# First mixer of a decoder trunk: GpSimd without products and weight parts, triangles inverted in blocks of eight rows, weight parts 512 columns wide in three tiles

## The chip, the core and the metric

The kernel runs on one core of a Trainium2 chip. The core has TensorE (PE, with its weight loads shown apart as PEld), VectorE (DVE), ScalarE (ACT), GpSimd (POOL) and SyncE (SP, which issues the DMAs here). Each engine works through a queue of its own in order. The metric is device microseconds of one execution; lower is better. Times of instructions are from one profiled execution.

## What is computed

Two layers on x of 256 tokens by 2048: an RWKV-7 mixer, then differential attention, each followed by a gated MLP and by layer norms. The change is in the mixer. Cut to what matters:

```
xr, xw, xk, xv, xa, xg = (x + xx * mu[i] for i in range(6))     # xx: the token before, less x
r, k, v = xr @ w_rkv[0], xk @ w_rkv[1], xv @ w_rkv[2]
w = -softplus(-(w0 + tanh(xw @ w1) @ w2)) - 0.5
a = sigmoid(a0 + (xa @ a1) @ a2);   g = sigmoid(xg @ g1) @ g2
kk = normalized(k * k_k) per head;   k = k * (1 + (a - 1) * k_a);   decay = exp(-exp(w))
for t:  S = S * decay_t + (S a_t) b_t^T + v_t k_t^T;   y_t = S r_t     # a_t = -kk, b_t = kk * a
h = ((group_norm(y) * lnx_g + lnx_b + bonus) * g) @ w_o
```

Everything is float32. The step over t is not run token by token: the 256 tokens of a head are four chunks of 64, and in each chunk the effect of the (S a_t) b_t^T terms is the inverse of a triangular 64x64 matrix with ones on its diagonal.

## The kernel before

A float32 weight is cut into two parts in a rounded format, hi (an ACT cast of raw) and lo (raw less hi, a subtraction), and three products, hi with both parts of x and lo with the first, give a dense product on PE. `weights` (by way of `chunk`, L199) does it for a block of 128 outputs: one DMA brings `raw` with four k-tiles (512 columns), and for each HCH = 2 k-tiles (256 columns) ACT casts hi (L210) and DVE or POOL subtracts lo (L213). Where `pool_every` is n, every nth lo goes to POOL: every third in the first stage, every fourth in the groups. The tiles for raw, hi and lo come from rings; the ring "0" has (3, 4, 4) tiles, and the first stage has a second one, "v", with (6, 6, 6); blocks take turns between the rings that are open.

The first stage of the mixer (`rwkv`, to about 160 us) makes V from 16 blocks of weights, the first factors of the low-rank gates, and the mixes of x: for each mix and k-tile a product `mx` (L773) and a hi and lo part (L191, L192). Then the 32 heads go as 8 groups of four heads (two k-tiles), in a pipeline (`Groups.pipeline`): while group i is in `chain` (the recurrence over the four chunks) and `outputs`, group i+1 is in `lanes` (the triangles), i+2 in `front` (decays, normalization, the products AR, KB and M) and i+3 in `products` (its k and r, 4 blocks of 16 k-tiles). Near the end `early` puts part of w_o in the place of `products`. The generators are stepped by turns (`_together`, with the numbers of PACE), and the framework then sets the order of each engine's queue.

The steps that the change touches:

- POOL's products: Lx = L - sw (L1107), a = kk * a (L1122), one half of KB (L1130; DVE makes the other at L1129), r = r * k (L1159), KB times pc (L1198), and in `outputs` bon * rs (L1382) and V = y + bon (L1388).
- `lanes` inverts each triangle from the inside: the matrices go to DRAM and come back as `Ml`, one block of 16 rows to a partition and step; fifteen pairs of a product (L1209) and a reduce (L1211) on DVE fill Tl; Tl goes by DRAM to W1, 32 rows at a time. Then PE joins blocks of 16 into 32 (transpose L1227, matmuls L1233, copy to Z, matmuls L1240, copy to W1) and blocks of 32 into 64 (L1245 to L1267). The result stands in M, which `chain` reads.
- `chain` has for each chunk three hand-overs from PE and back: R (L1049), UV (L1049) and S (L1354).

Of the kernel before, what the change touches and what calls it, by code (L numbers as in the profile page):

```python
# [74 lines left out]
def _const_layout():  # L75
    at, n = {}, 0
    for name, w in (("ident", P), ("onesd", P)):
        at[name] = n
        n += w
    base = n  # L80
    for name, w in (("bd1", P), ("cent", P), ("mask", P), ("reset", T)):
# [12 lines left out]
def _constants():  # L94
    c = np.zeros((P, NCONST), np.float32)

    def put(name, a):
        c[:a.shape[0], CCOL[name]:CCOL[name] + a.shape[1]] = a

    eye = np.eye(P, dtype=np.float32)  # L100
    bd = np.kron(np.eye(2, dtype=np.float32), np.ones((64, 64), np.float32))
    put("ident", eye)
    put("bd1", bd)
    put("cent", eye - bd / 64)
    put("ones", np.ones((P, P), np.float32))
# [3 lines left out]
    put("mask", np.concatenate([s < t, s <= t], 1).astype(np.float32))  # L109
    reset = np.ones((P, T), np.float32)  # L110
# [12 lines left out]
    return c  # L123


class Trunk:
    def __init__(self, ctx, tc, a):
        self.ctx, self.tc, self.nc, self.a = ctx, tc, tc.nc, a
        nc = self.nc
# [18 lines left out]

    def weight_pools(self, ctx, name, bufs=(3, 4, 4)):
        w = tuple(ctx.enter_context(self.tc.tile_pool(name=f"{n}{name}", bufs=b))  # L150
                  for n, b in zip(("raw", "hi", "lo"), bufs))
        self.wp.append(w)
        ctx.callback(self.wp.remove, w)
# [46 lines left out]
    def chunk(self, src, k0, m, wp, pool=False):  # L200
        nc = self.nc
        wraw, whi, wlo = wp
        raw = wraw.tile([P, WCH * P], F32, name="raw")
        nc.sync.dma_start(out=raw[:, :m * P], in_=src[:, k0 * P:(k0 + m) * P])
        for k in range(0, m, HCH):
            s = min(HCH, m - k)
            r = raw[:, k * P:(k + s) * P]
            hi = whi.tile([P, HCH * P], F32R, name="hi")
            lo = wlo.tile([P, HCH * P], F32R, name="lo")
            nc.scalar.copy(out=hi[:, :s * P], in_=r)  # L210
            self.nw += 1
# [748 lines left out]
class Groups:  # L960
# [10 lines left out]
    def open(self):  # L971
# [103 lines left out]
    def front(self, g):  # L1075
# [51 lines left out]
        for par in range(2):  # L1127
            k_, a_, e_ = (self.half(x, par) for x in (ck, ca, ce))
            nc.vector.tensor_tensor(out=self.half(KB[:, :, par, :], par), in0=k_, in1=e_, op=ALU.mult)  # L1129
            nc.gpsimd.tensor_tensor(out=self.half(KB[:, :, 1 - par, :], par), in0=a_, in1=e_, op=ALU.mult)  # L1130
        nc.vector.scalar_tensor_tensor(out=AR[:, :, 0, :], in0=c3, scalar=-1.0, in1=_ch(_fl(Lx)), op0=ALU.mult,
# [26 lines left out]

        nc.gpsimd.tensor_tensor(out=r, in0=r, in1=k, op=ALU.mult)  # L1159
        for jj, j in js:  # L1160
# [17 lines left out]
    def lanes(self, g):  # L1178
# [15 lines left out]
        for q in range(2):  # L1194
            r = slice(64 * q, 64 * q + 64)
            nc.gpsimd.memset(Tl[r].rearrange("p a b -> p (a b)")[:, 8 * q:8 * q + 7 * 17 + 1:17], 1.0)

        nc.gpsimd.tensor_tensor(out=KB.rearrange("p c a s -> p c (a s)"), in0=KB.rearrange("p c a s -> p c (a s)"),  # L1198
                                in1=pc.rearrange("p j c o -> p (j c) o").broadcast_to([P, GT * NC, 2 * C]),
                                op=ALU.mult)  # L1200
        yield
        for u in range(0, GT * NC, 4):
# [11 lines left out]
        for q in range(2):  # L1214
            nc.sync.dma_start(out=self.dram(d2, 0, ((DBL, 64), (C, 8), (1, 16)), at=8 * C * q),
                              in_=Tl[64 * q:64 * q + 64])
        for par in range(2):
# [27 lines left out]
        nc.vector.transpose(out=T2.rearrange("p u t -> p (u t)"), in_=W1.rearrange("p u t -> p (u t)"))  # L1245
        Z2 = g1.tile([P, 8, 32], F32, name="Z2")
        ps = self.pst()
# [117 lines left out]
    def outputs(self, g):  # L1365
# [15 lines left out]
        nc.tensor.matmul(ps, lhsT=t.x("bd1"), rhs=_fl(y2), start=True, stop=True)  # L1381
        nc.gpsimd.tensor_tensor(out=bon, in0=bon, in1=rs, op=ALU.mult)  # L1382
        nc.vector.tensor_scalar(out=_fl(y2), in0=ps, scalar1=1.0 / 64, scalar2=GN_EPS, op0=ALU.mult, op1=ALU.add)
# [80 lines left out]
```

## Time and profile before

| | |
|---|---|
| timed runs, three | 2576.1 us median, 2573.64 to 2580.8 |
| the profiled execution | 2568.52 us, of which its span is 2566.5 |
| busy share of the span | PE 96%, DVE 80%, ACT 64%, POOL 15% |
| mean granted TensorE clock | 0.981 of 2.4 GHz |
| lo parts | 2984 on DVE, 144 on POOL |

The page gives busy shares over the whole span; the mixer is the first quarter of it and has other limits than the rest, so it is read by stretches. A matmul's end is modelled, so PE's busy time says little of how densely it is fed; the distance of starts says more.

### The profile page before, as it was taken

To read this page: it belongs to the slowest core of one execution; us is meant where nothing else is said; L and a number is where in the kernel's file an instruction comes from. 1 tells how busy PE (TensorE), PEld (TensorE's weight loads), DVE (VectorE), ACT (ScalarE), POOL (GpSimd) and SP (SyncE) were. 2 spreads that over 40 slices of the span, in tenths; PEclk is the share of its full clock that TensorE was granted. 3 is DMA by queue.
4 is the path that set the end of the run, shared out by engine and by line. 5 is a ranking of instruction groups with operands and counts; after the bars stand their busy time and mean duration, and the time that the engine had idled before them with its cause. 6 is when DMAs were issued, how large, how long until landed. Compare 5 with 4: busy or idle time off the path is not lost.

```text
span 2566.5 us, 54810 instructions
## 1 busy us (share of the span) xinstructions
PE 2468.5 (96%) x17598; PEld 2171.5 (85%) x17598; DVE 2053.8 (80%) x5100; ACT 1645.2 (64%) x4318; POOL 390.7 (15%) x456
## 2 busy tenths in 40 slices
PE   7999989899899999999999999999999999999996
PEld 6888778767788888888889899998888888888886
DVE  8977888887897777777777877779997777777776
ACT  5765555644576666666566766666676666666664
POOL 4343344332400000000111200003300000000111
PEclk9999999999999999999999999999999999999998
DMA  6544334344466555556766555556465555566664
GB/s 191 175 129 116 102 104 108 99 121 124 125 187 192 190 190 190 190 189 184 225 190 183 156 171 171 171 167 196 145 199 188 188 188 188 188 186 185 189 190 127
DMA packets 285186, 429.63 MB, mean 167 GB/s; under 512 B 69081, under 2 KB 91617, under 8 KB 284897
## 3 DMA queue, kind: packets, MB, share of 16 engines
q1 hardware_dynamic: 284896, 426.14, 55.0%
q8 instruction: 137, 2.24, 0.4%
q14 instruction: 153, 1.25, 0.2%
HBM read 421.03 MB, written 6.57 MB: 167 GB/s over the span
## 4 chain that ended last, share of the span: by engine, by line
PE 74%; DVE 4%; ACT 1%; issue 1%; DMA 1%; POOL 0%; ACTq 0%; DVEq 0%; SPq 0%; POOLq 0%
PE psd L225 42%; PE psd L226 21%; PE psd L293 1%; PE psd L291 1%; PE psd L292 1%; DVE lo L213 1%; PE psd L897 1%; PE psd L896 1%; PE psd L898 1%; PE lnst L345 1%; PE psd L221 1%; PE psd L223 1%; PE psd L222 1%; DMA raw<-in_rw_o 0%; PE pss L656 0%
## 5 line engine op out<-in xcount | busy, mean ns | idle before, releaser
L210 ACT CAST hi<-raw 128x256 fp32r<-128x256 f32 (+1 forms) x3128 | 1231.1, 405 | 676.5 <-PE psd L225 461.2
L213 DVE TENSOR_TENSOR lo<-raw,hi 128x256 fp32r<-128x256 f32 (+1 forms) x2984 | 1287.5, 442 | 404.4 <-ACT hi L210 369.4
L225 PE MATMUL psd<-S,hi 128*128 128x512 f32 x3004 | 1056.7, 396 | 0.4 <-ACT hi L210 0.4
L226 PE MATMUL psd<-S,lo 128*128 128x256 f32 x3004 | 842.2, 280 | 4.4 <-DVE lo L213 3.8
L225 PEld LDWEIGHTS psd<-S,hi 128*128 128x128 f32 x3004 | 566.0, 188 | 132.5 <-ACT hi L210 1.2
L226 PEld LDWEIGHTS psd<-S,lo 128*128 128x128 f32 x3004 | 565.8, 188 | 5.9 <-DVE lo L213 4.5
L225 PE MATMUL psd<-hs,hi 128*128 128x512 f32 x1290 | 451.4, 394 | 0.1
L226 PE MATMUL psd<-hs,lo 128*128 128x256 f32 x1290 | 361.5, 280 | 0.0
L225 PEld LDWEIGHTS psd<-hs,hi 128*128 128x128 f32 x1290 | 241.8, 187 | 56.5 <-ACT hi L210 1.0
L226 PEld LDWEIGHTS psd<-hs,lo 128*128 128x128 f32 x1290 | 243.1, 188 | 0.4 <-DVE lo L213 0.3
L363 POOL COPY ln_acc<-X 128x256 f32<-128x256 f32 x4 | 2.1, 528 | 1230.9 <-DVE X L397 1230.9
L213 POOL TENSOR_TENSOR lo<-raw,hi 128x256 fp32r<-128x256 f32 x144 | 130.4, 913 | 301.2 <-ACT hi L210 244.1
L223 PE MATMUL psd<-S,lo 128*128 128x256 f32 x480 | 140.6, 293 | 13.8 <-DVE lo L213 8.4
L221 PE MATMUL psd<-S,hi 128*128 128x256 f32 x480 | 141.6, 295 | 0.9 <-ACT hi L210 0.5
L222 PE MATMUL psd<-S,hi 128*128 128x256 f32 x480 | 141.4, 295 | 0.0
L223 PEld LDWEIGHTS psd<-S,lo 128*128 128x128 f32 x480 | 92.8, 193 | 22.3 <-DVE lo L213 12.8
L225 PE MATMUL psd<-S1r,hi 128*128 128x512 f32 x276 | 109.9, 427 | 1.4 <-ACT o_rs L1049 0.7
L370 POOL TENSOR_TENSOR ln_acc<-ln_acc,X 128x256 f32<-128x256 f32 x49 | 40.9, 834 | 402.4 <-DVE X L409 389.1
L221 PEld LDWEIGHTS psd<-S,hi 128*128 128x128 f32 x480 | 92.5, 193 | 5.7 <-ACT hi L210 1.5
L222 PEld LDWEIGHTS psd<-S,hi 128*128 128x128 f32 x480 | 92.8, 193 | 2.9 <-issue 2.7
L221 PE MATMUL psd<-S1r,hi 128*128 128x256 f32 x284 | 87.2, 307 | 1.4 <-ACT S1r L191 0.9
L897 PE MATMUL psd<-S,lo 128*128 128x258 f32 x256 | 75.4, 295 | 10.1 <-DVE lo L213 10.1
(297 smaller groups left out, 3823.5 us busy)
## 6 DMA issues: line engine op xcount, KB each, us to landing
raw<-in_ff_up SPq DMA_DIRECT2D x676, 256.0 KB, 3.4
raw<-in_ff_down SPq DMA_DIRECT2D x320, 256.0 KB, 3.0
raw<-in_rkv SPq DMA_DIRECT2D x192, 256.0 KB, 3.5
raw<-in_da_qk SPq DMA_DIRECT2D x122, 256.0 KB, 3.4
raw<-in_da_v SPq DMA_DIRECT2D x64, 256.0 KB, 3.1
raw<-in_da_o SPq DMA_DIRECT2D x64, 256.0 KB, 3.5
raw<-in_rw_o SPq DMA_DIRECT2D x50, 256.0 KB, 3.5
raw<-in_ff_down SPq DMA_DIRECT2D x32, 192.0 KB, 2.7
```

What stands on the lines that cost most here:

```text
L210: nc.scalar.copy(out=hi[:, :s * P], in_=r)
L213: eng.tensor_tensor(out=lo[:, :s * P], in0=r, in1=hi[:, :s * P].bitcast(F32), op=ALU.subtract)
L221: nc.tensor.matmul(ps[:, :T], lhsT=hi, rhs=xs[:, :T], start=first, stop=False)
L222: nc.tensor.matmul(ps[:, :T], lhsT=hi, rhs=xs[:, T:], start=False, stop=False)
L223: nc.tensor.matmul(ps[:, :T], lhsT=lo, rhs=xs[:, :T], start=False, stop=last)
L225: nc.tensor.matmul(ps, lhsT=hi, rhs=xs, start=first, stop=False)
L226: nc.tensor.matmul(ps[:, T:], lhsT=lo, rhs=xs[:, :T], start=False, stop=last)
L291: nc.tensor.matmul(o, lhsT=xh, rhs=hi, start=k == 0 and b == 0, stop=False)
L292: nc.tensor.matmul(o, lhsT=xh, rhs=lo, start=False, stop=False)
L293: nc.tensor.matmul(o, lhsT=xl, rhs=hi, start=False, stop=k == KT - 1 and b == T // P - 1)
L370: nc.gpsimd.tensor_tensor(out=self.ln_acc[:, hs], in0=self.ln_acc[:, hs], in1=t, op=ALU.add)
L897: nc.tensor.matmul(ps[:, 2:4 + T], lhsT=lo[:, w], rhs=x[:, 2:4 + T], start=False, stop=False)
```

## The change

- lo parts all go to DVE in the mixer (pool = pool0 = 0), apart from the first chunk of each of the two opening blocks.
- `chunk` takes its piece width from the ring: WIDE = 4 k-tiles (512 columns) for rings "0" and "v", with three hi and three lo tiles of that width in each. After the mixer's groups `span` is set to HCH, and the wide tiles of ring "0" are then filled in two pieces of 256 columns; the other rings stay as they were.
- The seven products on POOL are written for DVE. One of the copies of W1 into M moves from POOL to ACT.
- `lanes` inverts blocks of 8 rows: Ml comes in one DMA with half the elements in each partition, seven pairs of product and reduce remain, and one more joining step (8 into 16) is put in front: transpose T0, 32 matmuls, a masked copy to Z8 on DVE, 32 matmuls, a copy to W1 on ACT. Z2 shares the buffer of T1.

```
-PACE = dict(... pool=4, pool0=3, ... wc='PVVA', ... w0=(3, 4, 4), ... vw=(6, 6, 6), ...)
+WIDE = 4
+PACE = dict(... pool=0, pool0=0, ... wc='AVVA', ... w0=(3, 3, 3), ... vw=(6, 3, 3), ...)
...
-        for k in range(0, m, HCH):
-            s = min(HCH, m - k)
-            r = raw[:, k * P:(k + s) * P]
-            hi = whi.tile([P, HCH * P], F32R, name="hi")
-            lo = wlo.tile([P, HCH * P], F32R, name="lo")
-            nc.scalar.copy(out=hi[:, :s * P], in_=r)
...
+        for k in range(0, m, width):
+            hi = whi.tile([P, width * P], F32R, name="hi")
+            lo = wlo.tile([P, width * P], F32R, name="lo")
+            n = min(width, m - k)
+            step = min(width, self.span)
+            for i in range(0, n, step):
+                s = min(step, n - i)
+                r = raw[:, (k + i) * P:(k + i + s) * P]
+                h, l = (x[:, i * P:(i + s) * P] for x in (hi, lo))
+                nc.scalar.copy(out=h, in_=r)
...
-        nc.gpsimd.tensor_tensor(out=Lx, in0=L, in1=sw, op=ALU.subtract)
+        nc.vector.tensor_tensor(out=Lx, in0=L, in1=sw, op=ALU.subtract)
...
-        for q in range(2):
-            nc.sync.dma_start(out=Ml[64 * q:64 * q + 64], in_=self.dram(d1, 0, ((DBL, 64), (C, 16), (1, 16))))
-        nc.gpsimd.memset(Ml.rearrange("p a b -> p (a b)")[:, 0:256:17], 1.0)
...
+        nc.sync.dma_start(out=Ml, in_=self.dram(d1, 0, ((DBL // 2, P), (C, 8), (1, 8))))
...
-        for i in range(1, 16):
-            nc.vector.tensor_tensor(out=tt[:, :, :i + 1], in0=Tl[:, :, :i + 1],
-                                    in1=Ml[:, 0:i + 1, i].unsqueeze(1).broadcast_to([P, 8, i + 1]), op=ALU.mult)
-            nc.vector.tensor_reduce(out=Tl[:, :, i], in_=tt[:, :, :i + 1], axis=AX.X, op=ALU.add)
+        for i in range(1, 8):
+            nc.vector.tensor_tensor(out=tt[:, :i, :i], in0=Tl[:, :i, :i],
+                                    in1=Ml[:, 0:i, i].unsqueeze(1).broadcast_to([P, i, i]), op=ALU.mult)
+            nc.vector.tensor_reduce(out=Tl[:, :i, i], in_=tt[:, :i, :i], axis=AX.X, op=ALU.add)
...
+        nc.vector.transpose(out=T0.rearrange("p u t -> p (u t)"), in_=W1.rearrange("p u t -> p (u t)"))
...
+                nc.tensor.matmul(pv[r, u], lhsT=N[q][r, u, be:be + 32], rhs=T0v[r, u, :, 0, :], start=True, stop=True)
+        nc.vector.tensor_tensor(out=self.Z8[:, :, :, 0, :], in0=pv,
+                                in1=t.x("m8", 16).rearrange("p (b i) -> p b i", b=2).unsqueeze(1).broadcast_to([P, 8, 2, 8]),
+                                op=ALU.mult)
+        yield
...
+                nc.tensor.matmul(pv[r, u], lhsT=self.Z8[r, u].rearrange("p b k i -> p (b k i)"), rhs=W1v[r, u, :, 1, :],
+                                 start=True, stop=True)
+        nc.scalar.copy(out=W1v[:, :, :, 1, :], in_=pv)
```

POOL's queue at the program's start, before (L770 makes the differences xx, L213 lo parts):

```order
L770 TENSOR_TENSOR xx_109<-xz_108 128x256 x3
L213 TENSOR_TENSOR lo_140<-raw_137,hi_139 128x256
L213 TENSOR_TENSOR lo_146<-raw_143,hi_145 128x256
L770 TENSOR_TENSOR xx_109<-xz_108 128x256 x3
L213 TENSOR_TENSOR lo_184<-raw_137,hi_183 128x256
L770 TENSOR_TENSOR xx_109<-xz_108 128x256
L213 TENSOR_TENSOR lo_205<-raw_143,hi_204 128x256
```

The same place after, as far as the first clearing of Tl and UV, which belong to the groups:

```order
L781 TENSOR_TENSOR xx<-xz 128x256 x3
L224 TENSOR_TENSOR lo<-raw,hi 128x512 x2
L781 TENSOR_TENSOR xx<-xz 128x256 x9
L1210 MEMSET Tl 128x64
L1211 MEMSET Tl 128x8
L998 MEMSET UV 128x1024
```

The lo parts between and behind the xx steps are gone from this queue; in the groups only clearings and the copy of pc are left on it.

DVE's queue where the triangles of a middle group begin, before (T and Tl are the products and the inverse, M and Z belong to the group ahead):

```order
L1105 SCALAR_TENSOR_TENSOR L<-ext,wa 128x256
L1209 TENSOR_TENSOR T_4494<-Tl,Ml 128x8x2
L1211 TENSOR_REDUCE Tl<-T_4494 128x8
L1209 TENSOR_TENSOR T_4494<-Tl,Ml 128x8x3
L1254 COPY Z_4413<-pss 32x256
L1211 TENSOR_REDUCE Tl<-T_4494 128x8
L1209 TENSOR_TENSOR T_4494<-Tl,Ml 128x8x4
L1211 TENSOR_REDUCE Tl<-T_4494 128x8
L1209 TENSOR_TENSOR T_4494<-Tl,Ml 128x8x5
```

The same place after:

```order
L1126 TENSOR_TENSOR Lx<-L,wa 128x512
L1224 TENSOR_TENSOR T_4047<-Tl,Ml 128x1
L1226 TENSOR_REDUCE Tl<-T_4047 128x1
L1224 TENSOR_TENSOR T_4047<-Tl,Ml 128x2x2
L1184 TENSOR_TENSOR bon<-pss,X 128x512
L1302 COPY M<-pss 32x8x32
L1226 TENSOR_REDUCE Tl<-T_4047 128x2
L1224 TENSOR_TENSOR T_4047<-Tl,Ml 128x3x3
L1226 TENSOR_REDUCE Tl<-T_4047 128x3
L1224 TENSOR_TENSOR T_4047<-Tl,Ml 128x4x4
```

Lx, which was POOL's, now stands in DVE's queue ahead of them, the products are smaller, and the copy of Z2 that stood among them has gone ahead.

## Rows read from the trace of the kernel before

**Rows 1.** Windows: stretch, its length, busy us of PE, PEld, DVE, ACT, POOL, clock, DMA.
```profile
20.00:160.00 140.00, 126.91 (x950) 119.35 (x950) 137.62 (x308) 97.95 (x283) 56.59 (x65) 0.98 0.53 160
160.00:258.00 98.00, 90.80 (x808) 80.79 (x807) 68.94 (x150) 55.52 (x129) 36.60 (x44) 0.90 0.44 120
258.00:510.00 252.00, 229.12 (x3068) 196.27 (x3066) 219.68 (x525) 148.49 (x354) 97.81 (x110) 0.96 0.40 104
695.00:2566.00 1871.00, 1838.70 (x11068) 1633.24 (x11066) 1465.71 (x3715) 1238.74 (x3279) 136.34 (x156) 0.99 0.60 182
```
**Rows 2.** Timeline: start us, duration us, engine, line; two of PE, four of DVE.
```profile
101.08 0.28 PE L221 MATMUL psd<-S,hi 128*128 128x256 f32 x1
101.20 0.28 PE L222 MATMUL psd<-S,hi 128*128 128x256 f32 x1
...
99.63 0.42 DVE L213 TENSOR_TENSOR lo<-raw,hi 128x256 fp32r<-128x256 f32 x1
99.96 0.42 DVE L192 TENSOR_TENSOR S1r<-mx,S1r 128x256 fp32r<-128x256 f32 x1
...
402.94 0.68 DVE L1387 TENSOR_TENSOR o_y<-o_y,o_rs 128x512 f32<-128x512 f32 x1
403.54 0.43 DVE L1245 STREAM_TRANSPOSE T<-W 128x256 f32<-128x256 f32 x1
```
**Rows 3.** Waits, 258 to 510 us: total us, times, longest us.
```profile
POOL Ml L1192 <- DMA Ml<-d: 15.8, 5, 6.2
...
PEld b L1327 <- DVE S L1354: 7.7, 5, 2.1
```
**Rows 4.** Groups by form, DVE, 700 to 2566 us: busy us, mean ns, idle before.
```profile
L321 DVE TENSOR_TENSOR rs_l<-ors 128x256 f32<-128x256 f32 x8 | 3.3, 418 | 0.0
...
L321 DVE TENSOR_TENSOR ln_m<-ln_rs 128x256 f32<-128x256 f32 x3 | 2.9, 950 | 0.0
```
**Rows 5.** Groups by form, 20 to 160 us: DVE, then POOL.
```profile
L213 DVE TENSOR_TENSOR lo<-raw,hi 128x256 fp32r<-128x256 f32 x120 | 54.5, 479 | 0.9 <-ACT hi L210 0.6
L773 DVE SCALAR_TENSOR_TENSOR mx<-xx,par,xz 128x256 f32<-128x256 f32 x88 | 53.0, 628 | 0.1
L192 DVE TENSOR_TENSOR S1r<-mx,S1r 128x256 fp32r<-128x256 f32 x64 | 29.9, 481 | 0.0
L192 DVE TENSOR_TENSOR S<-mx,S 128x256 fp32r<-128x256 f32 x24 | 12.1, 528 | 0.9 <-ACT S L191 0.8
...
L213 POOL TENSOR_TENSOR lo<-raw,hi 128x256 fp32r<-128x256 f32 x59 | 54.3, 936 | 79.7 <-ACT hi L210 63.9 <-PE psd L223 9.8 <-PE psd L222 4.1
```
**Rows 6.** One line, DVE, 0 to 640 us: ns min/median/max, first and last start.
```profile
L773 DVE SCALAR_TENSOR_TENSOR mx<-xx,par,xz x96: 468/477/977, 3.5 to 152.5; 128x256 f32<-128x256 f32 x96
...
L213 DVE TENSOR_TENSOR lo<-raw,hi x361: 401/418/1972, 23.5 to 636.7; 128x256 fp32r<-128x256 f32 x181
```
**Rows 7.** Groups by form, DVE, 258 to 510 us (five groups).
```profile
L213 DVE TENSOR_TENSOR lo<-raw,hi 128x256 fp32r<-128x256 f32 x117 | 58.8, 513 | 11.0 <-ACT hi L210 10.0
...
L1129 DVE TENSOR_TENSOR KB<-k,wa 128x256 f32<-128x256 f32 x10 | 9.8, 1008 | 0.0
...
L1227 DVE STREAM_TRANSPOSE T<-W 128x256 f32<-128x256 f32 x5 | 2.2, 439 | 0.1
...
L1209 DVE TENSOR_TENSOR T<-Tl,Ml 128x128 f32<-128x128 f32 x5 | 1.9, 373 | 0.0
...
L1209 DVE TENSOR_TENSOR T<-Tl,Ml 128x40 f32<-128x40 f32 x5 | 1.1, 228 | 0.2
```
**Rows 8.** Windows of DVE on line 1209, then on line 1211: busy us, clock, DMA.
```profile
258.00:510.00 252.00, 27.22 (x74) 0.96 0.40 104
258.00:510.00 252.00, 16.77 (x74) 0.96 0.40 104
```
**Rows 9.** Groups by form, 258 to 510 us: PE, then ACT.
```profile
L1240 PE MATMUL pss<-W,Z 32*32 32x16 f32 x320 | 3.6, 180 | 1.7 <-DVE Z L1049 1.7
...
L210 ACT CAST hi<-raw 128x256 fp32r<-128x256 f32 x156 | 60.1, 405 | 56.4 <-PE psd L222 37.1 <-DMA raw<-in_rkv 11.3 <-PE psd L223 5.0
```

More of the change, by code (lines that the diff above doesn't have):

```diff
@@ L80, in _const_layout @@
     base = n
-    for name, w in (("bd1", P), ("cent", P), ("mask", P), ("reset", T)):
+    for name, w in (("bd1", P), ("cent", P), ("mask", P), ("reset", T), ("m8", 16)):
         at[name] = n
@@ L109, in _constants @@
     put("mask", np.concatenate([s < t, s <= t], 1).astype(np.float32))
+    m8 = np.ones((P, 16), np.float32)
+    m8[np.arange(P) % 32 >= 24, :8] = 0
+    put("m8", m8)
     reset = np.ones((P, T), np.float32)
@@ L133, in __init__ @@
         self.wp = []
-        self.weight_pools(ctx, "0", PACE["w0"])
+        self.span = WIDE
+        self.weight_pools(ctx, "0", PACE["w0"], WIDE)
         self.tmp = mk("tmp", 3)
@@ L147, in c, with weight_pools @@
         return self.cst[:rows, CCOL[name]:CCOL[name] + w]
-    def weight_pools(self, ctx, name, bufs=(3, 4, 4)):
+    def weight_pools(self, ctx, name, bufs=(3, 4, 4), width=HCH):
         w = tuple(ctx.enter_context(self.tc.tile_pool(name=f"{n}{name}", bufs=b))
-                  for n, b in zip(("raw", "hi", "lo"), bufs))
+                  for n, b in zip(("raw", "hi", "lo"), bufs)) + (width,)
         self.wp.append(w)
@@ L805, in rwkv @@
             self.pool_every = 0
+            self.span = HCH
             self.weight_pools(ctx, "o")
@@ L991, in open @@
             nc.gpsimd.tensor_copy(out=self.Z[r, :, 16:], in_=t.cst[r, o:o + 16].unsqueeze(1).broadcast_to([32, 8, 16]))
+        self.Z8 = fx.tile([P, 8, 2, 2, 8], F32, name="Z8")
+        for q in range(4):
+            r = slice(32 * q, 32 * q + 32)
+            for b in range(2):
+                o = CCOL["ident"] + 32 * q + 16 * b + 8
+                nc.gpsimd.tensor_copy(out=self.Z8[r, :, b, 1, :],
+                                      in_=t.cst[r, o:o + 8].unsqueeze(1).broadcast_to([32, 8, 8]))
         self.d2 = d2p.tile([P, DBL * 64 // P], F32, name="d2")
@@ L1129, in front @@
             nc.vector.tensor_tensor(out=self.half(KB[:, :, par, :], par), in0=k_, in1=e_, op=ALU.mult)
-            nc.gpsimd.tensor_tensor(out=self.half(KB[:, :, 1 - par, :], par), in0=a_, in1=e_, op=ALU.mult)
+            nc.vector.tensor_tensor(out=self.half(KB[:, :, 1 - par, :], par), in0=a_, in1=e_, op=ALU.mult)
         nc.vector.scalar_tensor_tensor(out=AR[:, :, 0, :], in0=c3, scalar=-1.0, in1=_ch(_fl(Lx)), op0=ALU.mult,
@@ L1157, in front @@
             yield from self.gates(g + 1)
-        nc.gpsimd.tensor_tensor(out=r, in0=r, in1=k, op=ALU.mult)
+        nc.vector.tensor_tensor(out=r, in0=r, in1=k, op=ALU.mult)
         for jj, j in js:
@@ L1188, in lanes @@
         Z = self.Z
-        for q in range(2):
-            nc.sync.dma_start(out=Ml[64 * q:64 * q + 64], in_=self.dram(d1, 0, ((DBL, 64), (C, 16), (1, 16))))
-        nc.gpsimd.memset(Ml.rearrange("p a b -> p (a b)")[:, 0:256:17], 1.0)
+        nc.sync.dma_start(out=Ml, in_=self.dram(d1, 0, ((DBL // 2, P), (C, 8), (1, 8))))
         nc.gpsimd.memset(Tl, 0.0)
[L1194 to L1198, printed above, removed]
+        nc.gpsimd.memset(Tl.rearrange("p a b -> p (a b)")[:, 0:64:9], 1.0)
+        nc.vector.tensor_tensor(out=KB.rearrange("p c a s -> p c (a s)"), in0=KB.rearrange("p c a s -> p c (a s)"),
                                 in1=pc.rearrange("p j c o -> p (j c) o").broadcast_to([P, GT * NC, 2 * C]),
@@ L1225, in lanes @@
         N = [self.units(M, 1)] * 2 + [self.units(M, 0)] * 2
+        T0 = g1.tile([P, 8, 32], F32, name="T1")
+        nc.vector.transpose(out=T0.rearrange("p u t -> p (u t)"), in_=W1.rearrange("p u t -> p (u t)"))
+        T0v, W1v = (x.rearrange("p u (b k i) -> p u b k i", b=2, k=2) for x in (T0, W1))
+        ps = self.pst()
+        pv = ps[:, :P].rearrange("p (u b i) -> p u b i", b=2, i=8)
+        for u in range(8):
+            for q, r in enumerate(rows):
+                be = 32 * (q % 2)
+                nc.tensor.matmul(pv[r, u], lhsT=N[q][r, u, be:be + 32], rhs=T0v[r, u, :, 0, :], start=True, stop=True)
[3 more added lines that the diff above has]
+        yield
+        ps = self.pst()
+        pv = ps[:, :P].rearrange("p (u b i) -> p u b i", b=2, i=8)
+        for u in range(8):
+            for r in rows:
+                nc.tensor.matmul(pv[r, u], lhsT=self.Z8[r, u].rearrange("p b k i -> p (b k i)"), rhs=W1v[r, u, :, 1, :],
+                                 start=True, stop=True)
+        nc.scalar.copy(out=W1v[:, :, :, 1, :], in_=pv)
+        yield
         T1 = g1.tile([P, 8, 32], F32, name="T1")
@@ L1245, in lanes @@
         nc.vector.transpose(out=T2.rearrange("p u t -> p (u t)"), in_=W1.rearrange("p u t -> p (u t)"))
-        Z2 = g1.tile([P, 8, 32], F32, name="Z2")
+        Z2 = g1.tile([P, 8, 32], F32, name="T1")
         ps = self.pst()
@@ L1381, in outputs @@
         nc.tensor.matmul(ps, lhsT=t.x("bd1"), rhs=_fl(y2), start=True, stop=True)
-        nc.gpsimd.tensor_tensor(out=bon, in0=bon, in1=rs, op=ALU.mult)
+        nc.vector.tensor_tensor(out=bon, in0=bon, in1=rs, op=ALU.mult)
         nc.vector.tensor_scalar(out=_fl(y2), in0=ps, scalar1=1.0 / 64, scalar2=GN_EPS, op0=ALU.mult, op1=ALU.add)
@@ L1387, in outputs @@
         nc.vector.tensor_tensor(out=y, in0=y, in1=rs, op=ALU.mult)
-        nc.gpsimd.tensor_tensor(out=self.V[:, j0:j0 + GT, :], in0=y, in1=bon, op=ALU.add)
+        nc.vector.tensor_tensor(out=self.V[:, j0:j0 + GT, :], in0=y, in1=bon, op=ALU.add)
         if g >= NG - 3:
```

28 lines of the change are left out of this document (13 added, 15 removed).

## The prediction

> **What bounds the kernel now.** I read the windows first: they cut the span into stages and give each engine's busy time and the granted clock of each [rows 1]. From 695 us on, PE is busy 1838.7 of 1871 us at a clock of 0.99; the change hardly reaches there, since those stages keep pieces of 256 columns. The first mixer, 0 to 695 us, is where it acts. In its first stage (20 to 160 us: the V blocks, the low-rank factors, the mixing of x) VectorE (DVE) is busy 137.6 of 140 us, so DVE sets that stage. In the five steady groups (258 to 510 us, 50.4 us each) DVE is busy 219.7 of 252, GpSimd (POOL) 97.8, ScalarE (ACT) 148.5, and PE 229.1. PE's busy time deceives: its matmuls of 256 columns are recorded with 0.28 us but start 0.12 us apart [rows 2], so much of what reads as busy is the tail of a matmul that nothing follows. The waits say who is late: PE's loads stand still for DVE's S, by up to 2.1 us at a time [rows 3], a small step of the recurrence that comes off one in-order DVE queue. So I take DVE as the bound of the first stage, and DVE's queue with PE's short waits for it as the bound of the groups.
>
> **What POOL costs DVE.** The same instruction, L321 on 128x256, takes 418 ns in one place and 950 in another [rows 4]; the slow ones run beside POOL's centring of X. In the mixer the median of mx (477) and of lo (418) is the undisturbed time [rows 6], and the means of the first stage lie above it [rows 5]; S1r and S are the same kind of instruction as lo, so 418 is theirs too. Times their counts: mx 88 x 0.151 = 13.3, S1r 64 x 0.063 = 4.0, S 24 x 0.110 = 2.6, lo 120 x 0.061 = 7.3, together 27.2 us that DVE loses to 54.3 us of POOL work: half of it. The Trainium skill (SBUF — State Buffer, Who interferes with whom) holds that a GpSimd instruction that reads SBUF and a DVE instruction with two SBUF inputs lock each other out for a whole instruction; were all 54.3 us of POOL's time lost to DVE, the stage would gain 27 us more than these rows say. The measured half decides.
>
> **Pace.** DVE instructions overlap a little, so I count from start to start: 99.63 to 99.96 gives 0.335 us for 256 columns, and 402.94 to 403.54 gives 0.605 for 512 [rows 2], each within 0.005. One piece of 512 instead of two of 256 saves 0.065.
>
> **First stage.** DVE makes 120 lo pieces and POOL 59 [rows 5]. After, DVE makes all 179 as 89.5 wide ones: 89.5 x 0.605 = 54.1 against 120 x 0.335 = 40.2, that is +13.9. POOL keeps the early xx steps and two lo pieces ahead of this window, so I give back all 27.2. Net -13.3 of 137.6. Next late is PE: 950 matmuls x 0.12 = 114 us, below the 124 left, so DVE stays the bound and the gain shows nearly whole: **-13 us** (bounds 0, if loads or ACT are next, and -20, if PE also gets rid of its waits). ACT has 42 of 140 us idle and gets half as many casts of twice the width: nothing.
>
> **Each steady group.** Four items on DVE, in us per group.
> - Contention goes. Shown [rows 7]: lo 117 x (513 - 418) = 11.1 and KB 10 x (1008 - 418) = 5.9, DVE and POOL making one half each side by side; the triangles' products 27.2 [rows 8], of which 15 x 5 x 0.275 = 20.6 is undisturbed (228 ns for 40 columns, 373 for 128 [rows 7]), so 6.6. Sum 23.6, 4.7 per group. By the first stage's half, POOL's 97.8 us would cost 49, 9.8 per group. Between these ends I take **-5.7**, nearer to what rows show.
> - POOL's products come over: five of 512 columns (Lx, wa, r, bon, X) at 0.605, 3.0; two KB halves at 0.335, 0.7; KB times pc with 1024 columns, estimated from the two paces as 0.605 + 2 x 0.27 = 1.1. **+4.8**.
> - Weight parts: a group has 4 x 16 k-tiles, 32 halves, of which POOL makes every fourth. 24 x 0.335 = 8.0 become 16 x 0.605 = 9.7. **+1.7**.
> - Triangles: fifteen products undisturbed are 4.1, fifteen reduces 16.8 / 5 = 3.4 [rows 8], 7.5 in all. Seven pairs remain with 1 to 49 columns, 0.4 a pair by the 228 ns of 40 columns and the mean reduce (16.77 / 74 = 0.23), so 2.8. The new block step adds one transpose (439 ns [rows 7]) and one masked copy of half its columns, some 0.3: 3.5. **-4.0**.
>
> Net **-3.2** on DVE per group, 43.9 becoming 40.7. PE gets 64 tiny matmuls more per group: 32 of them have 3.6 / 5 = 0.7 us of busy time [rows 9]; the two added hand-overs are spread among dense matmuls, as the old ones are, so I charge 0.3 (bounds 0 and 1.5). One small copy of W1 moves from POOL to ACT, which is idle 41% of the time: nothing. hi and lo grow from 8 to 12 k-tiles of lookahead; ACT's casts, which now stop 37.1 us for buffers that PE still reads [rows 9], get further ahead, which I put at -0.3 (bounds 0 and -2). The two DMAs that fetch Ml become one, and DVE waits for it directly where POOL did; POOL stood up to 6.2 us for it [rows 3], but DVE reaches that row later than POOL, so 0 (bounds 0 and +2). Steady groups: 5 x -3.2 = **-16**.
>
> **The rest.** In the two groups of the fill, 160 to 258 us, DVE is busy 68.9 of 98 us [rows 1]; waits that aren't DVE's end last there more often, so I take half a group's gain each, and the same for the three of the drain: **-3** and **-5**. From 630 us on only the number of wide tiles changes: 0. The clock, 0.90 and 0.96 in fill and groups [rows 1], I leave where it is.
>
> Sum: -13 - 16 - 3 - 5 = **-37 us**. The profiled execution took 2568.5 us (span 2566.5), so 2531.5 for one like it; the three timed runs have the median 2576.1, 7.6 above it, and the same difference gives **2539**.
>
> **Rivals.**
> - *DVE held up more than its own time.* With shorter steps and deeper lookahead, half of DVE's idle time in the groups (32 us) goes as well: -16 there, -7 in fill and drain, -5 in the first stage: 2511. For it: where DVE waits it is for ACT and PE, which a faster DVE serves sooner. Against: the order of the queues is fixed when the program is built, and ACT still stops for PE's buffers.
> - *The hand-overs of the recurrence bound the groups.* PE to DVE to PE takes its time whatever DVE's load; the groups stay at 50.4 us and only the first stage gains: 2563. For it: DVE is idle 13% of the groups as it is. Against: PE's waits are for DVE by name.
> - *Nothing much.* The first stage too finds another bound at once (the loads of raw, or PE's clock) and gains 4 us at most: 2572.
> - *Slower: long pieces before short steps.* Some 16 steps of a group (four each of R, UV, S and the triangles') are handed to DVE and awaited by PE. Each now finds pieces of 0.605 instead of 0.335 us ahead of it, and POOL's products too. At 0.2 us more for each, the group's 3.2 are gone; at the whole length, 0.6, it is 16 x 0.6 - 3.2 = +6.4 a group, 8 groups +51, less 13 in the first stage: 2614. The kernel gets slower from about 0.3 us a step. Against: before, the same steps met lo pieces disturbed up to 1.97 us [rows 6]. The Trainium skill (Perfetto Trace Analysis, Optimizing Scalar/DVE Operations) advises breaking instructions up where an engine that isn't full leaves bubbles on another; by that rule the groups would go this way, and no row of before has a wide lo piece to show it.
>
> That the change doesn't do what it says is out: in POOL's new order two lo pieces and the xx steps are all that is left of its products.
>
> **How the numbers follow.** Forecast 2539, 0.48 (2523 to 2556 with its bounds); more 0.17; hand-overs 0.15; nothing 0.10; slower 0.10. A measurement of this kernel can tell 0.3%, 8 us, from no change. Faster by that (below 2568) are the first three, 0.80; within it the fourth, 0.10; slower the last, 0.10. The range leaves out the slower case and a sliver at the fast end: 2510 to 2572.
>
> **What would show it.** Right: the first stage's DVE time falls by some 13 us and the last V block ends that much sooner; wide lo rows show one time near 0.69 us with mean and median alike; the spacing of the groups falls from 50.4 to about 47; PE's waits for S shrink. Wrong: spacing unchanged with DVE under 80% busy (hand-overs), or longer waits of PE for R, UV and S behind wide lo rows (long pieces). A stage after 695 us that moves by more than 5 us would be outside of what I reckoned.

## The result, and the profile after

The changed kernel takes 2549.6 us (median of four, 2543.0 to 2550.4) beside 2576.8 for the kernel before: a ratio of 0.9888, interval 0.9864 to 0.9911, so 27 us or 1.1% faster. The profiled execution took 2549.88 us, its span 2548.0, 18.5 less than the span of before. The forecast was 2539, its range 2510 to 2572.

The windows of the changed kernel, in the stretches of [rows 1] (busy us of PE, PEld, DVE, ACT, POOL, clock, DMA):

```profile
20.00:160.00 140.00, 133.96 (x1028) 128.35 (x1029) 127.85 (x286) 92.64 (x204) 4.50 (x15) 0.98 0.59 175
160.00:258.00 98.00, 89.88 (x1016) 79.14 (x1015) 75.19 (x162) 54.84 (x104) 1.47 (x7) 0.97 0.44 118
258.00:510.00 252.00, 241.58 (x3725) 203.90 (x3723) 200.59 (x456) 141.55 (x292) 3.23 (x15) 0.95 0.38 100
695.00:2548.00 1853.00, 1824.25 (x10941) 1616.12 (x10939) 1418.07 (x3675) 1163.53 (x3247) 122.16 (x143) 1.00 0.62 183
```

DVE falls from 137.62 to 127.85 in the first stage and from 219.68 to 200.59 in the groups. Fixed stretches hide the shift, though: a stage that ends sooner moves into the next window. So the program is cut at its own events: the recurrence's first matmul, the first matmul of `outputs` of group 0 and of group 5 (five groups between them), and the end of the first layer's norm. The kernel before:

```profile
0.00:167.00 167.00, 143.28 (x1034) 132.34 (x1035) 151.31 (x331) 106.65 (x305) 70.63 (x90) 0.98 0.56 174
167.00:292.20 125.20, 115.47 (x1097) 102.06 (x1096) 97.59 (x223) 71.77 (x170) 47.94 (x53) 0.90 0.42 113
292.20:548.30 256.10, 235.06 (x3063) 194.93 (x3061) 221.47 (x536) 149.81 (x359) 95.34 (x106) 0.95 0.39 103
548.30:691.40 143.10, 132.40 (x1316) 105.31 (x1315) 115.04 (x294) 75.38 (x199) 37.58 (x49) 0.96 0.46 133
```

The changed kernel, the same four stages:

```profile
0.00:157.90 157.90, 139.29 (x1039) 132.52 (x1040) 137.75 (x301) 97.34 (x212) 15.93 (x34) 0.98 0.61 184
157.90:278.40 120.50, 111.98 (x1416) 98.55 (x1415) 91.31 (x193) 65.11 (x126) 1.47 (x7) 0.97 0.44 120
278.40:533.00 254.60, 242.08 (x3575) 201.98 (x3573) 203.11 (x467) 142.05 (x293) 3.23 (x15) 0.93 0.38 101
533.00:671.70 138.70, 130.82 (x1508) 104.48 (x1507) 113.35 (x272) 71.91 (x172) 12.66 (x19) 0.99 0.46 133
```

The first stage is 9.1 us shorter, the fill 4.7, the five groups only 1.5, drain and norm 4.4; what follows is 1.2 longer. In the groups DVE gave up 18.4 us and the time didn't follow. The clock column matters too: 0.90 became 0.97 in the fill, while the groups fell from 0.95 to 0.93. A mean of 0.93 over 254.6 us is 36 us at 1.2 instead of 2.4 GHz. In what follows, length times clock is called the length at the full clock: 243.3 before and 236.8 after for the five groups. It supposes that PE sets the pace of the stretch. Where PE doesn't, it takes off too much: over the 85 executions behind this document, compared within each kernel, one microsecond more of span times (1 - clock) went with 0.53 us more of span, and with 0.35 in the kernel before. So a difference between two such lengths with unlike clocks is an estimate.

The prices of DVE in the first stage came out as read, by form (busy us, mean ns, idle before):

```profile
L224 DVE TENSOR_TENSOR lo<-raw,hi 128x512 fp32r<-128x512 f32 x93 | 61.9, 684 | 6.7 <-ACT hi L221 6.6
L784 DVE SCALAR_TENSOR_TENSOR mx<-xx,par,xz 128x256 f32<-128x256 f32 x88 | 40.1, 477 | 0.0
L199 DVE TENSOR_TENSOR S1r<-mx,S1r 128x256 fp32r<-128x256 f32 x64 | 25.7, 417 | 0.9 <-ACT S1r L198 0.9
L199 DVE TENSOR_TENSOR S<-mx,S 128x256 fp32r<-128x256 f32 x25 | 9.7, 415 | 1.5 <-ACT S L198 1.5
```

Beside [rows 5], mx fell from 628 to 477, S1r from 481 to 417, S from 528 to 415: the lengthening was GpSimd's doing and is gone.

### The profile page after: what moved, and what is told of

It reads as the page before. It is cut to its first block, busy times and chain, and to the rows that moved or that the text cites. A ratio compares the mean times of both kernels' runs of the same rounds, so it can differ in the third digit from the quotient of the medians.

```text
span 2548.0 us, 54661 instructions
## 1 busy us (share of the span) xinstructions
PE 2470.0 (97%) x18626; PEld 2174.2 (85%) x18626; DVE 1985.9 (78%) x4948; ACT 1554.3 (61%) x4088; POOL 169.2 (7%) x234
## 4 chain that ended last, share of the span: by engine, by line
PE 85%; DVE 6%; DMA 4%; ACT 3%; issue 1%; SPq 0%; ACTq 0%; POOL 0%; DVEq 0%; POOLq 0%
PE psd L236 43%; PE psd L237 22%; PE psd L232 3%; PE psd L234 3%; PE psd L233 3%; DVE lo L224 2%; PE psd L303 1%; PE psd L304 1%; PE psd L302 1%; DMA raw<-in_rkv 1%; ACT hi L221 1%; DMA raw<-in_rw_o 1%; DMA raw<-in_ff_up 1%; PE psd L909 1%; PE lnst L356 1%
## 5 line engine op out<-in xcount | busy, mean ns | idle before, releaser
L221 ACT CAST hi<-raw 128x256 fp32r<-128x256 f32 (+1 forms) x2882 | 1132.4, 422 | 786.4 <-PE psd L236 540.1
L224 DVE TENSOR_TENSOR lo<-raw,hi 128x256 fp32r<-128x256 f32 (+1 forms) x2880 | 1222.7, 455 | 444.3 <-ACT hi L221 421.2
L236 PE MATMUL psd<-S1a,hi 128*128 128x512 f32 x240 | 84.9, 398 | 0.0
L537 DVE SCALAR_TENSOR_TENSOR gc<-gp,cpar,gc 128x256 f32<-128x256 f32 x172 | 82.6, 480 | 2.6
```

Of the source, the lines that this page charges most:

```text
L221: nc.scalar.copy(out=h, in_=r)
L224: eng.tensor_tensor(out=l, in0=r, in1=h.bitcast(F32), op=ALU.subtract)
L236: nc.tensor.matmul(ps, lhsT=hi, rhs=xs, start=first, stop=False)
L537: nc.vector.scalar_tensor_tensor(out=gc, in0=g[:, k:k + T], scalar=cw(k, j), in1=gc, op0=ALU.mult, op1=ALU.add)
```

## The experiments

Three theories stood at the start. *DVE*: its load sets the groups, as predicted. *PE*: its own work does. *Hand-overs*: the way from PE to another engine and back does, whatever the loads. The runs were made in three comparisons, each with its own runs of the kernel before (medians 2568.1, 2573.9 and 2571.0); ratios are to those, that of the first profile of the changed kernel to 2576.8. "Groups part" is fill, five groups, drain and norm, each at the full clock and summed; it is known to some 3 us.

| run | ratio | start of recurrence, us | five groups: us, clock | groups part |
|---|---|---|---|---|
| before, profiled | 1 | 167.0 | 256.1, 0.95 | 493.4 |
| changed, profiled | 0.9888 | 157.9 | 254.6, 0.93 | 491.0 |
| r_after | 0.9884 | 158.4 | 243.5, 0.98 | 493.2 |
| e1_dve_load | 0.9911 | 158.6 | 246.9, 0.97 | 497.3 |
| e2_pe_less | 0.9900 | 156.7 | 242.8, 0.90 | 472.0 |
| e3_tri16 | 0.9923 | 156.9 | 253.3, 0.96 | 495.1 |
| e4_pool_products | 0.9944 | 157.0 | 254.5, 0.96 | 503.0 |
| e5_narrow | 0.9869 | 161.1 | 244.8, 0.96 | 492.6 |
| e6_pool_lo | 0.9961 | 166.4 | 246.2, 0.97 | 496.3 |
| e8_first_only | 0.9938 | 157.4 | 245.3, 0.99 | 502.9 |
| b1_dve_load | 1.0031 | 166.9 | 262.8, 0.93 | 506.4 |
| e9_fill | 0.9868 | 157.3 | 243.6, 0.98 | 494.6 |
| e10_v_less | 0.9931 | 166.2 | 250.4, 0.94 | 487.9 |
| e11_narrow_groups | 0.9893 | 157.2 | 240.2, 0.98 | 490.8 |

**More work for DVE.** The changed kernel with eight reduces a group that nothing reads:

```
+        load = lambda n: [nc.vector.tensor_reduce(out=self.dm[:, i:i + 1], in_=_fl(r), axis=AX.X, op=ALU.add) for i in range(n)]
...
+        load(2)      # at four places of front
```

> The changed kernel with eight more DVE instructions in each group: reductions of 512 columns that nobody reads, 0.6 us each, 4.8 us a group. DVE is busy 40 of 51 us in a steady group of the changed kernel. Theory PE (PE's own queue sets the spacing of the groups now): spacing stays 51 to 52 us, the whole kernel at most 6 us slower. Theory DVE (DVE's queue still sets it): spacing rises by most of 4.8 to 55 or 56, the kernel 30 to 40 us slower. Theory hand-overs (PE to DVE to PE latency sets it): each hand-over waits a little longer, 1 to 2 us a group, 8 to 16 us in all.

The added row by form, and then the window of the five groups of this run:

```profile
L1108 DVE TENSOR_REDUCE dm<-r 128x1 f32<-128x512 f32 x40 | 26.3, 675 | 0.1
```

```profile
276.80:523.70 246.90, 236.01 (x3558) 198.68 (x3557) 217.99 (x503) 139.90 (x287) 2.83 (x15) 0.97 0.36 100
```

DVE did 26.3 us more in the five groups, and they take 239.5 us at the full clock beside 236.8: plus 2.7. DVE's load doesn't set them. Over all eight groups it is 64 reduces, 43 us; the whole, 0.9911 beside the changed kernel's 0.9886 (mean of its two), got some 6 us longer, far from the 30 to 40 of *DVE*. That is the edge of what *PE* gave, at most 6, and less than the 8 to 16 of *hand-overs*, so between these two it doesn't decide.

**Less work for PE.** In groups 3 to 7 the product of hi with the low part of x is left out of k and r, 64 matmuls a group; the result is less exact there.

```
-            nc.tensor.matmul(ps[:, :T], lhsT=hi, rhs=xs[:, T:], start=False, stop=False)
+            if not two:
+                nc.tensor.matmul(ps[:, :T], lhsT=hi, rhs=xs[:, T:], start=False, stop=False)
...
```

> The changed kernel without the second of the three products (hi times the low part of x) in k and r of groups 3 to 7, so that 64 matmuls of 256 columns are missing in each of five steady groups, 64 x 0.118 = 7.5 us of PE; this leaves out a part of the computation. Theory PE: spacing falls from 51.4 to 44 or 45, the kernel is 30 to 37 us faster than the changed one. Theory DVE and theory hand-overs: spacing falls by 0 to 2 us, the kernel by at most 10.

```profile
269.10:511.90 242.80, 224.18 (x3234) 180.56 (x3233) 196.88 (x463) 137.21 (x289) 2.74 (x15) 0.90 0.38 103
```

5 x 64 x 0.118 = 37.8 us of matmuls went. At the full clock the groups part falls by 19 to 21, half of it. Measured, the five groups lose 11.8 against the first profile of the changed kernel and only 0.7 against the second, with the clock at 0.90. The whole, 0.9900 (0.9871 to 0.9930) beside 0.9886, gained nothing, where *PE* gave 30 to 37 us and the other two at most 10. So PE's work sets at most about half of the groups' length, by an estimate that takes the half clock off in full; that it sets half is not shown. Part of the rest is a new wait in the five groups (us in all, times, longest), where the second profile of the changed kernel has 0.4 us:

```profile
PE psd L232 <- ACT hi L221: 10.5, 8, 2.9
```

**The parts taken back.** First the triangles of sixteen rows (seven pairs and the added join undone), then the seven products on GpSimd:

```
-        nc.vector.tensor_tensor(out=Lx, in0=L, in1=sw, op=ALU.subtract)
+        nc.gpsimd.tensor_tensor(out=Lx, in0=L, in1=sw, op=ALU.subtract)
...
```

> The changed kernel with the triangles inverted in blocks of 16 rows again, all else kept: PE loses 64 small matmuls and two hand-overs a group (0.65 us for each 32 in the trace of the changed kernel, 1.3), DVE gains 4. Theory PE: spacing 49.5 to 51, the kernel 3 to 12 us faster than the changed one. Theory DVE: spacing 54 to 55, 25 to 30 us slower. Theory hand-overs: two fewer, 2 to 3 us a group, 15 to 25 us faster.

> The changed kernel with its seven products of a group on POOL again (lo parts all on DVE and wide as in the changed kernel): DVE loses 4.8 us of work a group and pays again for POOL's 12 us, at half of it 6. Theory PE: spacing moves by less than 1 us, the kernel by less than 6. Theory DVE: +1 us a group, 8 us slower. Theory hand-overs: POOL's products take 1.3 to 2.0 us instead of 0.6, which shows where a later step waits for them, 1 to 2 us a group slower.

Without the new triangles the ratio is 0.9923, interval 0.9905 to 0.9940, 9 us worse than the changed kernel's 0.9886, with the groups part 3 longer at the full clock. None of the three theories had that: *PE* and *hand-overs* forecast gains from two hand-overs fewer, *DVE* 25 to 30 us more. With the products on GpSimd it is 0.9944 (0.9928 to 0.9960), 15 worse, and the groups part 10 to 12 longer: more than the 6 of *PE* and the 8 of *DVE*, and within the 8 to 16 of *hand-overs*. Taken with the two runs before, no one theory holds.

**The changed kernel once more, pieces of 256, GpSimd's lo parts, and only the first stage.** These four shared one comparison.

```
-WIDE = 4                          # e5: rings of (3, 4, 4) and (6, 6, 6) with it
+WIDE = 2
...
-pool=0, pool0=0                   # e6
+pool=4, pool0=3
...
-pool=0, pool0=0, wc='AVVA'        # e8, with the edits of e3 and e4
+pool=4, pool0=0, wc='PVVA'
```

> The changed kernel once more, as a base beside the next three. If the half-clock stretches are part of the program, its five steady groups again show some 34 us at half clock and take 254 to 255 us, and the whole 2543 to 2550. If they come by chance, the length of the groups moves with them, by half a microsecond for each at half clock; at 14 us (as in the run with more DVE work) the groups would take 245.

> The changed kernel with pieces of 256 columns again (rings of 3, 4, 4 and 6, 6, 6 tiles). DVE and ACT get two instructions for each piece, 0.065 us more a pair on DVE: 6 us in the first stage, 1 a group. If PE sets both (theory PE), nothing shows: V ends at 158 to 159 us, the five groups take 253 to 256, 2550 in all. If DVE's load sets them, plus 6 and plus 1 a group: 2563. If the long pieces stand in the way of the recurrence's steps, the groups get shorter by 1 to 3 us each: 2535 to 2545.

> The changed kernel with GpSimd making every third lo part of the first stage and every fourth of the groups, as before but 512 columns wide. First stage: DVE loses some 18 us of lo parts to GpSimd and gets back the slower mx, S1r and lo; by the prediction's account DVE is at 138 us again and the first chunk's start of the recurrence goes from 158 to about 166. If PE set the first stage of the kernel before as well, it stays at 158. Groups: theory PE gives 0 to plus 1 each (a wide lo part takes near 1.9 us on GpSimd). In all 2557 by the first, 2550 by the second.

> The changed kernel with everything that acts in the groups undone: products on GpSimd, triangles of sixteen rows, every fourth lo part of the groups on GpSimd; what is left is the first stage without GpSimd and the wide pieces. If the gain is the first stage's, the recurrence starts at 158 us and the groups take 255 to 258: 2552 to 2558. If the changes in the groups carry what I predicted for them and something else hid it, the loss is 16 and 8 more: 2570.

The same program, profiled again (0.9884, 0.9866 to 0.9902):

```profile
0.00:158.40 158.40, 140.05 (x1039) 132.45 (x1040) 137.75 (x301) 97.37 (x212) 15.71 (x34) 1.00 0.60 183
158.40:275.80 117.40, 109.00 (x1417) 96.18 (x1416) 91.21 (x193) 65.00 (x126) 1.16 (x7) 1.00 0.44 123
275.80:519.30 243.50, 232.12 (x3575) 194.81 (x3573) 202.73 (x467) 141.91 (x293) 3.23 (x15) 0.98 0.39 106
519.30:659.30 140.00, 131.78 (x1507) 105.28 (x1506) 113.41 (x272) 71.94 (x172) 12.63 (x19) 0.98 0.45 132
```

The instruction counts and DVE's time are those of the first profile, and the five groups are 11.1 us shorter, with the clock at 0.98 instead of 0.93. At the full clock they agree: 238.6 and 236.8. The half-clock stretches are thus no fixed part of the program, and one profile of it says little of the groups' length. Over its eight executions the whole took 2537 to 2550 us at mean clocks of 0.985 to 0.993; the 27 of the kernel before in the three comparisons lie at 0.978 to 0.985.

Narrow pieces (0.9869, 0.9853 to 0.9886) start the recurrence 2.7 to 3.2 us later and lose nothing after it: wide pieces bring a little in the first stage and stand in nobody's way in the groups of the changed kernel. GpSimd's lo parts (0.9961, 0.9946 to 0.9976) bring mx to 684 ns and the start back to 166.4, as expected of DVE as the bound; PE itself stands only 2.0 us for GpSimd's lo there (by form, 20 to 166 us):

```profile
L784 DVE SCALAR_TENSOR_TENSOR mx<-xx,par,xz 128x256 f32<-128x256 f32 x87 | 56.6, 684 | 0.1
...
L224 POOL TENSOR_TENSOR lo<-raw,hi 128x512 fp32r<-128x512 f32 x29 | 47.7, 1648 | 88.2 <-ACT hi L221 78.2 <-PE psd L234 4.8 <-DMA raw<-in_rkv 3.8
```

Their fill, and that of the first-stage-only kernel, in that order:

```profile
166.40:292.40 126.00, 115.01 (x1417) 101.29 (x1416) 87.72 (x181) 65.01 (x126) 21.43 (x19) 0.93 0.42 115
```

```profile
157.40:281.60 124.20, 107.78 (x1096) 96.63 (x1095) 88.79 (x189) 63.93 (x123) 48.67 (x43) 0.95 0.41 115
```

The four kernels in which GpSimd makes lo parts in the groups have a fill at 0.90 to 0.95 (before 0.90, b1 0.92); the ten other profiles have 0.96 to 1.00. The first stage alone gives 0.9938 (0.9923 to 0.9953): the edits in the groups are worth the 13 us from there to 0.9886. But its groups part, 502.9, is 9.5 longer than that of the kernel before, from which it differs there by the wide pieces and by the buffer that Z2 shares. In time it is no longer, 522.3 beside 524.4. In its fill PE stands for GpSimd's wide lo parts, 8.8 us in three waits, where the kernel before has 3.2 and the run with GpSimd's lo parts 4.0:

```profile
PE psd L234 <- POOL lo L224: 8.8, 3, 4.9
```

That wide pieces cost this beside GpSimd's work and nothing without it is how it looks; no run isolates it, and the parts taken back one by one don't add up to the whole.

**More work for DVE in the kernel before, and three more of the changed kernel.** b1 is the edit of e1. e9 puts dense matmuls whose result is overwritten ahead of the last two joins, where PE has tiny matmuls and then waits; e10 leaves hi with the low part of x out of 14 blocks of V; e11 fills the wide tiles in two pieces from the groups on.

```
+        if g < 5:                                  # e9, twice
+            for i in range(8):
+                nc.tensor.matmul(ps[:, :T], lhsT=t.S0[:, i % KT, :P], rhs=t.S0[:, i % KT, :T], start=True, stop=True)
...
+                self.span = HCH                    # e11, behind gr.open()
```

> The kernel before with the same additional DVE work as in the first run: eight reduces of 512 columns a group, 0.6 us each, nothing reads them. If DVE's queue set the steady groups of before, as I predicted, each gets near 5 us longer, the five 20 to 25 (242 us, taken at the full clock, become 262 to 267), with fill and drain 30 to 40 in all: 2605. If PE set them already then, the five stay at 240 to 246 at the full clock, and the whole within 10 us of the kernel before.

The added work in the kernel before, by form from 290 to 550 us, and the window of its five groups, which hold one reduce more:

```profile
L1089 DVE TENSOR_REDUCE dm<-r 128x1 f32<-128x512 f32 x39 | 26.0, 675 | 0.1
```

```profile
297.30:560.10 262.80, 242.47 (x3063) 197.40 (x3061) 230.79 (x572) 148.94 (x358) 88.43 (x104) 0.93 0.37 99
```

26.7 us more for DVE leave the five groups at 244.4 us at the full clock, plus 1.1, and in time plus 6.7. The whole is 1.0031 (1.0015 to 1.0046), 8 us for 43 us of added work; at the full clock the fill got 7.3 longer (112.7 to 120.0) and drain and norm 4.6. DVE's load didn't set the groups of the kernel before either. The test is less clean here: GpSimd's product r has to wait for the reduces that read r, 17.5 us in the five groups, so some of the 8 us may be GpSimd's.

> The changed kernel with eight more dense matmuls of 256 columns, whose results are overwritten, ahead of each of the last two joins of the triangles, in groups 0 to 4: 16 x 0.118 = 1.9 us of PE a group, put where PE otherwise does tiny matmuls and waits, just ahead of where the clock falls. If that thin place is what lets the clock fall, the half-clock time in the five groups goes from 10 to 34 us to under 7, and they take 240 to 246 in spite of 9.4 us more work. If the place has nothing to do with it, half-clock time stays at 10 to 34 us and the groups get 5 to 9 us longer.

```profile
275.40:519.00 243.60, 238.88 (x3638) 202.25 (x3637) 202.32 (x467) 142.26 (x293) 3.57 (x15) 0.98 0.39 106
```

Eighty more dense matmuls, 9.4 us of PE, 64 of them in this window, and the five groups stay as they were in the better profile of the changed kernel. That profile's clock, 0.98, doesn't decide what I expected of it. The executions say more: all four took 2535.2 to 2536.6 us, at clocks of 0.992 to 0.995. The ratio is 0.9868 (0.9854 to 0.9883), the lowest here along with the narrow pieces; its interval overlaps that of the changed kernel, so it is not shown to be faster, only not slower for more work, and at a steadier clock.

> The changed kernel without the product of hi and the low part of x in 14 of the 16 blocks of V: 14 x 16 = 224 matmuls at 0.118 us, 26 us of PE in the first stage (V is less exact, nothing else changes). If PE sets that stage now, the first product of the recurrence comes 8 to 13 us sooner (145 to 150 us), until DVE's 127 us stop it. If DVE still sets it, as I predicted, or the loads of raw do, it stays at 155 to 158.

```profile
PE psd L235 <- DVE lo L224: 19.2, 23, 2.0
ACT hi L221 <- DMA raw<-in_rkv: 19.1, 21, 3.2
```

A miss: 26 us less for PE, and the start comes 8 us later, 166.2, not sooner. These waits of 20 to 166 us (us in all, times, longest) show PE standing for DVE's lo and ACT for raw; the clock of the stage is 0.96. In the second profile of the changed kernel, 20 to 160 us, PE stands 4.3 us for DVE's lo and ACT 7.5 us for raw. So PE's work alone doesn't set the first stage. Why it got longer isn't settled; 0.04 of 166.2, 7 us, is what the clock could account for.

> The changed kernel with the wide tiles filled in two pieces of 256 columns from the groups on; the first stage keeps pieces of 512. If the shorter pieces of the narrow run are what made its drain and groups a little shorter, and the wide ones its first stage 3 us longer, this takes both gains: recurrence from 158 us, five groups 238 at the full clock, 2536 to 2541. If the narrow run was better by chance of the clock alone, 2545 as the changed kernel.

Start 157.2, and 0.9893 (0.9878 to 0.9908), no better than the changed kernel: the narrow pieces' small advantage was chance, or comes from their other rings.

## Why the prediction was right, and where it was wrong

The sign and the size held, by a sum whose largest term was wrong and was replaced by one that I had left out, so the nearness of the number is luck. Of the 18.5 us between the two profiled spans, 9.1 are the first stage, 2.4 the groups part at the full clock (493.4 to 491.0), and 8.2 less loss at the half clock (524.4 - 493.4 = 31.0 before, 513.8 - 491.0 = 22.8 after); what follows took 1.2 more. By the second profile of the changed kernel it is 8.6, 0.2 and 23.3, less 0.9, of 31.2. The share of the half clock counts it in full; by the 0.53 above it would be about half of that, and the difference the groups'. So the first stage's share is shown, and how the rest divides between the groups and the clock is not.

- **First stage, -13: measured -9.1.** DVE as its bound in the kernel before holds: with lo parts back on GpSimd it lasts as long as before, and emptying PE doesn't shorten it. DVE's work fell from 151.31 to 137.75 us up to the start of the recurrence, 13.6 where I reckoned 13.3. That GpSimd costs DVE half of its own time, not all, held as well: by the rule of the Trainium skill that I set beside the row (SBUF — State Buffer, Who interferes with whom), read as the loss of all of GpSimd's time, 27 us more would have gone. Failed: "the gain shows nearly whole". Twenty-us windows, the kernel before and then the changed one:

```profile
20.00:40.00 20.00, 15.45 (x93) 13.65 (x92) 19.44 (x44) 14.35 (x42) 8.17 (x10) 0.83 0.44 131
40.00:60.00 20.00, 18.08 (x132) 16.70 (x133) 20.00 (x47) 12.45 (x35) 7.81 (x8) 1.00 0.53 157
```

```profile
20.00:40.00 20.00, 16.67 (x94) 14.57 (x95) 17.04 (x41) 12.31 (x29) 0.00 (x0) 0.83 0.47 140
40.00:60.00 20.00, 17.41 (x132) 16.34 (x131) 17.16 (x38) 10.74 (x25) 0.00 (x0) 1.00 0.60 166
...
140.00:160.00 20.00, 20.00 (x168) 19.40 (x167) 14.55 (x28) 9.50 (x20) 4.50 (x15) 1.00 0.54 148
```

DVE now idles 5.8 us between 20 and 60, where it idled 0.6: the lo rows above wait 6.6 us for ACT's hi. That is enough for the 4.5 us by which the stage's gain, 9.1, falls short of DVE's 13.6. At the end PE is full: 168 matmuls in 20 us, one each 0.119. My floor of 114 us for PE rested on the 950 matmuls from 20 to 160 us, but the stage goes on to 167: cut at its event it has 1034 matmuls before and 1039 after, of which some 1010 lie behind 20 us, 121 us at 0.12. What bounds the stage in the changed kernel is open: with PE's work cut (e10) it lasted 166.2 us with DVE busy 139.16 and PE 125.45.

- **Steady groups, -16: measured -1.5 and, in the second profile, -12.6; at the full clock -5 to -6.5.** The term's own sum was right, DVE lost 18.4 us there. What failed is the step ahead of it, "DVE's queue with PE's short waits for it as the bound of the groups": 26 us more for DVE cost 1 to 3 us at the full clock, in either kernel, and no more than 6.7 in time. What sets the groups instead stays open, as the runs e1 to e4 fit no one theory. PE's waits for S did go, as I said they would: 7.7 us before [rows 3], none among the longest in the second profile of the changed kernel, where the longest of PE's waits in the five groups is one in the joins:

```profile
PE pss L1295 <- ACT T L1288: 4.3, 5, 0.9
```

A wait that ends on DVE is no proof that DVE's load made it; DVE's step may itself have come late from PE.
- **Products on GpSimd, contention.** KB, 1008 ns for a half in [rows 7], is at 422 and 419, and KB times pc at 1219 where I had estimated 1.1 us:

```profile
L1213 DVE TENSOR_TENSOR KB<-KB,pc 128x1024 f32<-128x1024 f32 x5 | 6.1, 1219 | 0.0
...
L1148 DVE TENSOR_TENSOR KB<-k,wa 128x256 f32<-128x256 f32 x8 | 3.4, 422 | 0.1
L1149 DVE TENSOR_TENSOR KB<-wa 128x256 f32<-128x256 f32 x8 | 3.3, 419 | 0.0
```

- **ACT's lookahead, -0.3 a group:** no sign of it. ACT's casts stop 59.9 us for PE's buffers in 258 to 510 us, where they stopped 37.1 [rows 9].
- **Fill -3, drain -5: measured -4.7 and -4.4**, and -7.8 and -3.1 in the second profile. At the full clock the fill is 4 us longer (112.7 to 116.9) and the drain unchanged (137.4 to 137.3). That the clock could be left where it is failed: the fill went from 0.90 to 0.97 and 1.00 in the kernel in which GpSimd makes no lo parts, and drain and norm from 0.96 to 0.99 and 0.98.
- **After 695 us, 0: measured +1.2** from the first layer's norm on. Right.
- **The rivals.** By the first profile the groups went as *the hand-overs* said, spacing 51.2 to 50.9 us with DVE at 80%; by the second the spacing is 48.7. The time of 2563 did not come, and the mean clock was higher. That hand-overs set the groups isn't shown: two fewer of them a group (e3) brought no gain. *Long pieces*: the narrow pieces gain nothing after the start. *Nothing much* and *DVE held up more*: no sign.

## What to carry to other kernels

Before an engine's saved time is booked as the kernel's, load that engine with work that nothing reads: two lines showed here that 43 us of DVE over eight groups cost 6 to 8 us of the whole, and a wait that names an engine doesn't show it. Compare stages at their own events and with the granted clock beside each length, and profile the same program twice before a difference of a few microseconds in a stage is given a cause. What PE has free in a chain of short steps could be filled with dense matmuls at no cost in time here (e9), and the clock was steadier for it.

## What was not expected of the hardware

In these runs less work for PE came with more half clock, which gave part of the gain back: with 37.8 us of matmuls less the five groups ran at 0.90; with 9.4 us more, all four executions as a whole stayed at 0.992 or above, where the changed kernel has 0.985 to 0.993. In the changed kernel the clock falls, among other places, at the triangles' last join (the second window below lies wholly at 1.2 GHz; the line behind them is from PE's timeline: start, length, and in brackets the idle time before it):

```profile
334.00:338.00 4.00, 3.44 (x42) 2.99 (x43) 3.87 (x9) 3.90 (x8) 0.00 (x0) 0.69 0.12 33
338.00:342.00 4.00, 4.00 (x13) 2.50 (x11) 2.26 (x9) 2.60 (x6) 0.00 (x0) 0.50 0.01 4
```

```profile
334.30 0.24 PE L1295 MATMUL pss<-W,T 32*32 32x32 f32 x2 [0.87 <-ACT T L1288]
```

The Trainium skill (TensorE: Matmul & The Clock Gate, HAM oscillation) holds that gaps of PE between bursts send the clock back to half. Here PE stands 0.87 us for ACT's T ahead of the join, its longest stop from 326 us until the clock falls; the first row still reads busy 3.44 of 4 us, so busy time alone doesn't show such a gap.
